# A one-core expert kernel: the pair's weighted one-hot made at its beginning, transposed inside the gate product, and the last pair's combines two k-tiles later

## The chip, the cores and the metric

The kernel runs on one core of a Trainium2 chip. The metric is the device time of one launch in microseconds (us). TensorE (PE) multiplies, VectorE (DVE), ScalarE (ACT) and GpSimd (POOL) work on tiles, SyncE (SP) issues transfers (DMA). PEld is TensorE's weight load.

## The reference

A first block of two layers and then a second block of two layers, on 256 tokens of width 1024. The change lies in the second block's expert part, which runs once in each of its two layers:

```python
def grouped_moe(h, router_w, router_bias, w_gate, w_up, w_down):
    ...
    dense_gates = jnp.einsum('nk,nke->ne', gates, jax.nn.one_hot(idx, N_EXPERTS, dtype=F32)).astype(h.dtype)
    y = jnp.zeros_like(h)
    for e in range(N_EXPERTS):
        a = jax.nn.silu(h @ w_gate[e]) * (h @ w_up[e])
        y = y + dense_gates[:, e:e + 1] * (a @ w_down[e])
    return y
```

There are 16 experts of width 512, and each token goes to two of them. All weights are float32.

## The kernel before

In `moe(l, turn)` the experts are taken in 8 pairs, and each expert of a pair has 64 slots for its tokens, so that a pair fills the 128 rows of a tile. The steps of a pair, with their lines:

- `one_hot(g, pos)` (L1546, DVE) makes a one-hot `oh` of token against slot for a group of four experts. `gather` (L1562 on PE, L1564 on ACT) multiplies it with the tokens and gives `xg`, the tokens of each slot, in 8 steps. It runs for the even pairs; an odd pair uses the same `oh` and `xg`. Some steps run ahead of the pair, the others between the k-tiles of its gate product, by the argument `more` of `proj`.
- `proj` (L1597, PE) is every product with expert weights: `pg` (gate) and `pu` (up) over `KD` = 8 k-tiles, then down over 4 k-tiles for each part of the output columns: two halves of 512, or four quarters of 256 in the last pair. Each k-tile is a matmul for each of the two experts, which work side by side in column halves of the array; the trace has two passes for each, so four matmuls.
- The activation: tanh (L1632, ACT), two products (L1633, L1634, DVE), four transposes of `a` (L1638, PE), the copy to `aT` (L1640, ACT), which the down product needs.
- `combine_T(p, oh)`: the one-hot times the token's gate (`go`, L1607, DVE, two instructions), two transposes of it (L1612, PE), and from these `got`, the 0/1 matrix of slot against token (L1615, DVE), and `gs`, the gate of each slot (L1616, DVE).
- Each part of the down product is scaled by `gs` when it is evicted: `yh` (L1671, ACT) and the rest `yl` (L1672, DVE).
- `combine` (L1655, PE) multiplies `yh` and `yl` with `got` and adds that to the state `y` (L1657, DVE). For pairs 0 to 6 it is put on the list `steps`, and `pump()` runs one part of it at each call in the next pair. In the last pair (the one with `done`, which also takes the statistics of L802) it is called by `proj` between two k-tiles, through the argument `mid`.

TensorE follows the order in which the code is written. On the other engines a scheduler sets the order, and each then works strictly in it. Weights come in slots of 1 MB from a ring of 18 or more; SP issues them (L1683) in the order of use. PSUM has four banks for products (`mm_bank`) and four for transposes and combines (`at_bank`). The loop behind the pairs (L1716) is for experts with over 64 tokens, and does not run with these inputs.

Of the kernel before, what the change touches and what calls it, by code (L numbers as in the profile page):

```python
# [23 lines left out]
KD = D // P  # L24
# [51 lines left out]
def kernel(ctx: ExitStack, tc: tile.TileContext, A, const, out):  # L76
# [15 lines left out]
    def nm(s):  # L92
        cnt[0] += 1
        return f"{s}_{cnt[0]}"

    def t512(dt=F32):
        return tmp.tile([P, 512], dt, tag="t", name=nm("t"))

    def small(w):
        return sml.tile([P, w], F32, tag=f"s{w}", name=nm("s"))  # L100

    def mm_bank():
        return pmm.tile([P, 512], F32, tag="mm", name=nm("mm"))

    def at_bank():
        return pat.tile([P, 512], F32, tag="at", name=nm("at"))
# [3 lines left out]
    def pump(n=1):  # L110

        while posts:
            posts.pop(0)()
        while n and steps:
            if next(steps[0], False) is False:
                steps.pop(0)
            else:
                n -= 1
# [389 lines left out]
    def warm(func, dep):  # L508

        S.activation(small(2)[:, 0:1], dep, func, scale=0.0, bias=epst[:, 1:2])  # L510
# [964 lines left out]
    def moe(l, turn):  # L1475
# [15 lines left out]
        done = S.activation(sc, sc, AF.Tanh, scale=0.5)  # L1491
# [17 lines left out]
        gs, key, ing, mx = [small(8).rearrange("p (a g) -> p a g", a=2) for _ in range(4)]  # L1509
# [33 lines left out]
        def one_hot(g, pos):  # L1543
            oh = sml.tile([P, 2, 4 * SLOTS], F32R, tag="oh", name=nm("oh"), bufs=2)
            for i in range(2):
                V.tensor_tensor(oh[:, i].rearrange("p (e s) -> p e s", e=4),  # L1546
                                pos[:, i, 4 * g:4 * g + 4, None].to_broadcast([P, 4, SLOTS]),
                                C("count")[:, None, :].to_broadcast([P, 4, SLOTS]), op=OP.is_equal)
            return oh

        def gather(g, oh):

            xg = unit(U_PROB[(g + 1) % 2], "xg").rearrange("p (k s) -> p k s", k=KD)
            return xg, gather_steps(xg, oh)
# [12 lines left out]
        oh = one_hot(0, pos)  # L1567
        for i in range(2):
            last = V.tensor_sub(hn[1][:, i, 512:], y[:, i, 512:], hn[0][:, i, 512:])
        xg, more = gather(0, oh)  # L1570
# [20 lines left out]

        def proj(ps, lhs, ws, nk, mid=None, more=()):
            for k in range(nk):
                if mid and k == 1:
                    mid()
                for b in range(2):
                    PE.matmul(ps[64 * b:64 * b + 64, :], lhs(k, b), ws[k][b], start=k == 0, stop=k == nk - 1)  # L1597
                if k % 2:
                    for _ in range(2):
                        next(iter(more), None)  # L1600

        def combine_T(p, oh):

            go = t512()
            o = (p % 2) * P
            for i in range(2):
                V.tensor_tensor(go[:, i * P:(i + 1) * P].rearrange("p (e s) -> p e s", e=2),  # L1607
                                oh.bitcast(F32)[:, i, o:o + P].rearrange("p (e s) -> p e s", e=2),
                                gate[:, i, 2 * p:2 * p + 2, None].to_broadcast([P, 2, SLOTS]), op=OP.mult)
            pb = at_bank()  # L1610
            for i in range(2):
                PE.transpose(pb[:, i * P:(i + 1) * P], go[:, i * P:(i + 1) * P], ident)  # L1612
            got = sml.tile([P, T], F32R, tag="got", name=nm("got"), bufs=2)
            gs = small(2)
            V.tensor_scalar(got, pb[:, :T], 0.0, None, op0=OP.is_gt)  # L1615
            V.reduce_max(gs[:, 0:1], pb[:, :T], axis=AX.X)  # L1616
            return got, gs[:, 0:1]

        def pair(p, xg, more, oh, wg, wu, wd, done=None):
            def xs(k, b):  # L1620
                o = ((2 * p + b) % 4) * SLOTS
                return xg[:, k, o:o + SLOTS]

            if done:
                got, gs = combine_T(p, oh)
            pg, pu = mm_bank(), mm_bank()
            proj(pg, xs, wg, KD, more=more)
            if done:
                pump(2)
            proj(pu, xs, wu, KD)  # L1630
            th, a = t512(), t512()
            S.activation(th, pg, AF.Tanh, scale=0.5)  # L1632
            V.scalar_tensor_tensor(th, th, 1.0, pg, op0=OP.add, op1=OP.mult)  # L1633
            V.scalar_tensor_tensor(a, th, 0.5, pu, op0=OP.mult, op1=OP.mult)  # L1634
            pump()
            pb = at_bank()
            for j in range(4):
                PE.transpose(pb[:, j * P:(j + 1) * P], a[:, j * P:(j + 1) * P], ident)  # L1638
            aT = t512()
            S.copy(aT, pb)  # L1640
            if done:
                warm(AF.Abs_reciprocal_sqrt, aT[:, 0:1])
            pump()
            if not done:
                got, gs = combine_T(p, oh)
            n = len(wd)
            w = D // n
            yos = []

            def combine():  # L1650
                for q, yo in enumerate(yos):
                    for i in range(2):
                        pc = at_bank()
                        for j, part in enumerate(yo):
                            PE.matmul(pc[:, :w], got[:, i * P:(i + 1) * P], part, start=j == 0, stop=j == 1)  # L1655
                        ys = y[:, i, w * q:w * q + w]
                        V.tensor_add(ys, ys, pc[:, :w])  # L1657
                        if done:
                            done(q, i, n=n)
                    yield  # L1660

            comb = combine()
            if not done:
                steps.append(comb)
            for q in range(n):
                pd_ = mm_bank()
                proj(pd_[:, :w], lambda k, b: aT[:, k * P + 64 * b:k * P + 64 * b + 64], wd[q], 4, lambda: done and q and next(comb))
                if w * q % 512 == 0:
                    yh, yl = t512(F32R), t512(F32R)
                sl = slice(w * q % 512, w * q % 512 + w)  # L1670
                S.activation(yh[:, sl], pd_[:, :w], AF.Copy, scale=gs)  # L1671
                V.scalar_tensor_tensor(yl[:, sl], pd_[:, :w], gs, yh[:, sl], op0=OP.mult, op1=OP.subtract)  # L1672
                yos.append((yh[:, sl], yl[:, sl]))
            if done:
                next(comb)
# [26 lines left out]
        for p in range(NPAIR):  # L1702
            if p % 2 == 0 and p > 0:
                oh = one_hot(p // 2, pos)
                xg, more = gather(p // 2, oh)
                for _ in range(4):
                    next(more)
            pair(p, xg, more, oh, *experts(p, p == NPAIR - 1), done=stats if p == NPAIR - 1 else None)
# [7 lines left out]
        with tc.For_i(1, rounds, 1):  # L1716
            V.tensor_scalar_add(pos2, pos2, -float(SLOTS))
            for p in range(NPAIR):
                if p % 2 == 0:
                    oh = one_hot(p // 2, pos2)  # L1720
                    xg, more = gather(p // 2, oh)
                    for _ in range(2):
                        next(more)
                pair(p, xg, more, oh, *experts(p))
            finish()
            for q in range(4):
                stats(q, new=False, n=4)
# [62 lines left out]
```

## Time and profile before

| | us |
|---|---|
| median of 3 runs (1618.51 to 1620.62) | 1619.72 |
| the profiled execution, its own time | 1618.68 |
| its span, first to last instruction | 1616.4 |
| PE busy | 1510.0 |
| PEld busy | 1092.7 |
| DVE busy | 976.5 |
| ACT busy | 736.3 |
| POOL busy | 251.8 |

Busy times are sums over the span, in which stages with different limits follow one another. The second block begins near 840 us (its first L1207 on ACT is at 843.7); the expert stages of the two layers lie at about 990 to 1220 us and 1372 to 1601 us, and the rest is the second block's attention part and the ends. In the expert stages the page shows DMA at 9 of 10 and over 400 GB/s; elsewhere it is lower. Matmuls are pipelined, so PE's busy time overstates what it does.

### The profile page before, as it was taken

How to read it: one execution, taken by the hardware profiler on the slowest of the kernel's cores; microseconds unless marked ns; L12 is line 12 of the kernel's file. 1: busy time of each engine (PE TensorE's matmuls, PEld its weight loads, DVE VectorE, ACT ScalarE, POOL GpSimd, SP SyncE). 2: the span in 40 equal slices, each digit the busy share in tenths (PEclk: the TensorE clock that was granted, in tenths of full speed). 3: DMA queues.
4: the chain of work that ended last, by engine and by line, in shares of the span. 5: the costliest groups of instructions: out<-in, count | busy, mean ns of one | idle time of the engine just before them, and what ended most of it. 6: DMA issues, size and time to landing. Idle time of an engine off the chain costs nothing. (4 is left out here: it accounts for less than half of the span.)

```text
span 1616.4 us, 24413 instructions
## 1 busy us (share of the span) xinstructions
PE 1510.0 (93%) x9211; PEld 1092.7 (68%) x9211; DVE 976.5 (60%) x1894; ACT 736.3 (46%) x1403; POOL 251.8 (16%) x279
## 2 busy tenths in 40 slices
PE   6999999999999999999989998999988998999996
PEld 5877888888887888888878775334437776344332
DVE  4869777777786767777557774322137767222224
ACT  3466645655456664556446664112115565111112
POOL 0334640001242363000003100000001210000000
PEclk9999999999999999999999998999998999999998
DMA  9766769557854675965526368999985558899992
GB/s 346 245 215 236 261 219 353 181 179 235 313 186 136 218 271 185 318 207 174 164 73 209 128 222 300 403 407 407 407 314 168 179 180 315 314 407 406 407 405 92
DMA packets 278476, 419.71 MB, mean 260 GB/s; under 512 B 12722, under 2 KB 147748, under 8 KB 278348
## 3 DMA queue, kind: packets, MB, share of 16 engines
q1 hardware_dynamic: 273052, 398.63, 69.5%
q0 software_dynamic: 5152, 19.14, 3.4%
q8 instruction: 77, 1.26, 0.3%
q14 instruction: 51, 0.42, 0.1%
q10 hardware_dynamic: 144, 0.26, 0.0%
HBM read 416.94 MB, written 1.05 MB: 259 GB/s over the span
## 5 line engine op out<-in xcount | busy, mean ns | idle before, releaser
L279 DVE TENSOR_TENSOR split<-raw,split 128x1024 fp32r<-128x1024 f32 (+4 forms) x330 | 411.7, 1251 | 114.3 <-ACT split L278 111.2
L289 PE MATMUL mm<-hl,split 128*128 128x512 f32 x1168 | 412.6, 397 | 0.0
L278 ACT CAST split<-raw 128x1024 fp32r<-128x1024 f32 (+4 forms) x330 | 328.7, 1000 | 131.6 <-PE mm L323 69.5
L290 PE MATMUL mm<-hl,split 128*128 128x256 f32 x1168 | 326.3, 279 | 1.0 <-DVE split L279 1.0
L289 PEld LDWEIGHTS mm<-hl,split 128*128 128x128 f32 x1168 | 219.0, 187 | 50.4 <-issue 0.7
L1597 PE MATMUL mm<-raw,xg 128*64 128x512 f32 x1024 | 230.9, 602 | 1.1 <-ACT xg L1564 1.1
L290 PEld LDWEIGHTS mm<-hl,split 128*128 128x128 f32 x1168 | 220.3, 189 | 1.5 <-DVE split L279 1.3
L1597 PEld LDWEIGHTS mm<-raw,xg 128*64 128x64 f32 x1024 | 71.5, 138 | 136.5 <-issue 118.7
L289 PE MATMUL mm<-ahl,split 128*128 128x512 f32 x352 | 123.4, 395 | 0.0
L306 ACT COPY t<-mm 128x256 f32<-128x256 f32 x152 | 56.4, 371 | 142.7 <-PE mm L290 133.7
L1597 PE MATMUL mm<-raw,t 128*64 128x512 f32 (+1 forms) x576 | 114.8, 549 | 1.4 <-ACT t L1640 1.4
L321 PE MATMUL mm<-split,hl 128*128 128x512 f32 (+4 forms) x272 | 102.3, 376 | 4.2 <-ACT split L278 3.2
L290 PE MATMUL mm<-ahl,split 128*128 128x256 f32 x352 | 98.3, 279 | 0.3 <-DVE split L279 0.3
L322 PE MATMUL mm<-split,hl 128*128 128x512 f32 (+4 forms) x272 | 96.4, 355 | 1.0 <-DVE split L279 1.0
L323 PE MATMUL mm<-split,hl 128*128 128x512 f32 (+4 forms) x272 | 96.4, 355 | 0.3 <-POOL hl L1210 0.2
L306 DVE TENSOR_TENSOR t<-mm,t 128x256 f32<-128x256 f32 x140 | 59.1, 422 | 47.9 <-ACT t L306 47.7
L1633 DVE SCALAR_TENSOR_TENSOR t<-t,mm 128x512 f32<-128x512 f32 x16 | 11.0, 686 | 123.3 <-ACT t L1632 123.3
L1597 PEld LDWEIGHTS mm<-raw,t 128*64 128x64 f32 x576 | 39.4, 137 | 63.8 <-issue 53.4
L1672 DVE SCALAR_TENSOR_TENSOR t<-mm,s,t 128x512 fp32r<-128x512 f32 (+1 forms) x36 | 24.9, 692 | 94.9 <-ACT t L1671 94.9
L1671 ACT ACTIVATE t<-mm,s 128x512 fp32r<-128x512 f32 (+1 forms) x36 | 23.0, 640 | 129.9 <-PE mm L1597 129.9
L289 PEld LDWEIGHTS mm<-ahl,split 128*128 128x128 f32 x352 | 66.0, 187 | 15.5 <-ACT t L1095 0.2
L1640 ACT COPY t<-at 128x512 f32<-128x512 f32 x16 | 9.4, 586 | 129.7 <-PE at L1638 129.7
(426 smaller groups left out, 2563.3 us busy)
## 6 DMA issues: line engine op xcount, KB each, us to landing
raw<-in_exp_w_gate_dram SPq DMA_DIRECT2D x128, 512.0 KB
raw<-in_exp_w_up_dram SPq DMA_DIRECT2D x128, 512.0 KB
raw<-in_exp_w_down_dram SPq DMA_DIRECT2D x128, 512.0 KB
raw<-in_w_in_dram SPq DMA_DIRECT2D x54, 1024.0 KB
raw<-in_w_ada_dram SPq DMA_DIRECT2D x30, 1024.0 KB
raw<-in_w_gate_dram SPq DMA_DIRECT2D x22, 1024.0 KB
raw<-in_w_up_dram SPq DMA_DIRECT2D x22, 1024.0 KB
ada<-in_w_ada_dram POOLq DMA_DIRECT2D x18, 1024.0 KB, 5.8
```

The costliest lines, as they stand in the source:

```text
L278: S.copy(h, src)
L279: V.tensor_sub(lo, src, h)
L289: PE.matmul(ps, h[:, k], x[k0 + k], start=first and k == 0, stop=False)
L290: PE.matmul(ps[:, :T], lo[:, k], x[k0 + k][:, :T], start=False, stop=last and k == K - 1)
L306: return S.copy(b[:, :T], ps[:, T:]), V.tensor_add(dst, ps[:, :T], b[:, :T])
L321: PE.matmul(ps[i][:, :n], xh, h[:, j], start=f, stop=False)
L322: PE.matmul(ps[i][:, :n], xh, lo[:, j], start=False, stop=False)
L323: PE.matmul(ps[i][:, :n], xl, h[:, j], start=False, stop=z)
L1597: PE.matmul(ps[64 * b:64 * b + 64, :], lhs(k, b), ws[k][b], start=k == 0, stop=k == nk - 1)
L1633: V.scalar_tensor_tensor(th, th, 1.0, pg, op0=OP.add, op1=OP.mult)
L1671: S.activation(yh[:, sl], pd_[:, :w], AF.Copy, scale=gs)
L1672: V.scalar_tensor_tensor(yl[:, sl], pd_[:, :w], gs, yh[:, sl], op0=OP.mult, op1=OP.subtract)
```

## The change

`combine_T` becomes a generator in two parts. The first part, `go`, is called at the beginning of every pair. The second part, the transposes with `got` and `gs`, is called by the gate product's `proj` through `mid`. And `mid` is now called ahead of the k-tile with k = 3, where it was k = 1; for the last pair's combines, which use the same argument, that is two k-tiles later. Line numbers behind L1607 grow by one to three.

```diff
@@ -1591,7 +1591,7 @@
         def proj(ps, lhs, ws, nk, mid=None, more=()):
             for k in range(nk):
-                if mid and k == 1:
+                if mid and k == 3:
                     mid()
@@ -1607,6 +1607,7 @@
                                 gate[:, i, 2 * p:2 * p + 2, None].to_broadcast([P, 2, SLOTS]), op=OP.mult)
+            yield
             pb = at_bank()
...
             V.reduce_max(gs[:, 0:1], pb[:, :T], axis=AX.X)
-            return got, gs[:, 0:1]
+            yield got, gs[:, 0:1]
...
-            if done:
-                got, gs = combine_T(p, oh)
+            turned = combine_T(p, oh)
+            next(turned)
+            box = []
             pg, pu = mm_bank(), mm_bank()
-            proj(pg, xs, wg, KD, more=more)
+            proj(pg, xs, wg, KD, lambda: box.extend(next(turned)), more)
+            got, gs = box
...
-            if not done:
-                got, gs = combine_T(p, oh)
```

TensorE in pair 1 of the first layer, before: the end of the up product (`mm_10422`), the combine of pair 0 (`at_10460` to `at_10479`) around the transposes of `a` (`at_10468`), then the transposes of the one-hot, and the first two k-tiles of the down product (`mm_10493`). Here a row x4 is two k-tiles.

```order
L1597 MATMUL mm_10422<-raw_10406,xg_10191 64x512 x4
L1655 MATMUL at_10460<-t_10368,got_10355 128x512
L1655 MATMUL at_10460<-t_10369,got_10355 128x512
L1655 MATMUL at_10464<-t_10368,got_10355 128x512
L1655 MATMUL at_10464<-t_10369,got_10355 128x512
L1638 MATMUL at_10468<-con,t_10456 128x128 x4
L1655 MATMUL at_10475<-t_10381,got_10355 128x512
L1655 MATMUL at_10475<-t_10382,got_10355 128x512
L1655 MATMUL at_10479<-t_10381,got_10355 128x512
L1655 MATMUL at_10479<-t_10382,got_10355 128x512
L1612 MATMUL at_10486<-con,t_10483 128x128 x2
L1597 MATMUL mm_10493<-raw_10409,t_10473 64x512 x4
```

The same pair of the change: first the beginning of its gate product (`mm_10424`), then the end of the same stretch as above.

```order
L1597 MATMUL mm_10424<-raw_10385,xg_10191 64x512 x4
L1597 MATMUL mm_10424<-raw_10388,xg_10191 64x512 x2
L1613 MATMUL at_10432<-con,t_10421 128x128 x2
L1597 MATMUL mm_10424<-raw_10388,xg_10191 64x512 x2
L1597 MATMUL mm_10424<-raw_10391,xg_10191 64x512 x4
```

```order
L1641 MATMUL at_10478<-con,t_10466 128x128 x4
L1656 MATMUL at_10485<-t_10381,got_10281 128x512
L1656 MATMUL at_10485<-t_10382,got_10281 128x512
L1656 MATMUL at_10489<-t_10381,got_10281 128x512
L1656 MATMUL at_10489<-t_10382,got_10281 128x512
L1597 MATMUL mm_10493<-raw_10409,t_10483 64x512 x4
```

The two transposes (L1612, now L1613) have moved from ahead of the down product to behind the third k-tile of the gate product.

VectorE from the evictions of pair 0 (`t_10369`, `t_10382`) on, before:

```order
L1672 SCALAR_TENSOR_TENSOR t_10369<-mm_10359,s_10356,t_10368 128x512
L1672 SCALAR_TENSOR_TENSOR t_10382<-mm_10372,s_10356,t_10381 128x512
L1633 SCALAR_TENSOR_TENSOR t_10455<-t_10455,mm_10421 128x512
L1634 SCALAR_TENSOR_TENSOR t_10456<-t_10455,mm_10422 128x512
L1657 TENSOR_TENSOR state_8374<-state_8374,at_10460 128x512
L1657 TENSOR_TENSOR state_8374<-state_8374,at_10464 128x512
L1657 TENSOR_TENSOR state_8374<-state_8374,at_10475 128x512
L1657 TENSOR_TENSOR state_8374<-state_8374,at_10479 128x512
L1607 TENSOR_TENSOR t_10483<-oh_10186,gate_10204 128x128 x2
L1546 TENSOR_TENSOR oh_10839<-pos_10184,con 128x256
L1615 TENSOR_SCALAR got_10489<-at_10486 128x256
L1616 TENSOR_REDUCE s_10490<-at_10486 128x1
```

And in the change:

```order
L1673 SCALAR_TENSOR_TENSOR t_10369<-mm_10359,s_10282,t_10368 128x512
L1673 SCALAR_TENSOR_TENSOR t_10382<-mm_10372,s_10282,t_10381 128x512
L1607 TENSOR_TENSOR t_10421<-oh_10186,gate_10204 128x128 x2
L1546 TENSOR_TENSOR oh_10839<-pos_10184,con 128x256 x2
L1616 TENSOR_SCALAR got_10435<-at_10432 128x256
L1617 TENSOR_REDUCE s_10436<-at_10432 128x1
L1636 SCALAR_TENSOR_TENSOR t_10465<-t_10465,mm_10424 128x512
L1637 SCALAR_TENSOR_TENSOR t_10466<-t_10465,mm_10425 128x512
L1658 TENSOR_TENSOR state_8374<-state_8374,at_10470 128x512
```

The weighted one-hot (L1607) has moved from behind the four state additions to right behind the previous pair's last eviction, and `got` and `gs` from behind the additions to ahead of the products with tanh.

TensorE in the last pair of the first layer, the first two quarters of its down product (`mm_11455`, `mm_11468`) and the first combine, before and then in the change; here a row x2 is one k-tile.

```order
L1597 MATMUL mm_11455<-raw_11369,t_11451 64x256 x8
L1597 MATMUL mm_11468<-raw_11372,t_11451 64x256 x2
L1655 MATMUL at_11471<-t_11464,got_11387 128x256
L1655 MATMUL at_11471<-t_11465,got_11387 128x256
L1655 MATMUL at_11477<-t_11464,got_11387 128x256
L1655 MATMUL at_11477<-t_11465,got_11387 128x256
L1597 MATMUL mm_11468<-raw_11372,t_11451 64x256 x6
```

```order
L1597 MATMUL mm_11455<-raw_11369,t_11451 64x256 x8
L1597 MATMUL mm_11468<-raw_11372,t_11451 64x256 x6
L1656 MATMUL at_11475<-t_11464,got_11395 128x256
L1656 MATMUL at_11475<-t_11465,got_11395 128x256
L1656 MATMUL at_11481<-t_11464,got_11395 128x256
L1656 MATMUL at_11481<-t_11465,got_11395 128x256
L1597 MATMUL mm_11468<-raw_11372,t_11451 64x256 x2
```

The combine of a quarter has moved from behind the first k-tile of the next quarter to behind its third. The last quarter's combine has no product behind it and stays where it was. ACT, POOL and SP have the same instructions in the same order.

## Rows read from the trace of the kernel before

**Rows 1.** Busy time by stretch: start:end us, length, PE, PEld, DVE, ACT, POOL, PEclk, DMA share, GB/s.

```profile
1020.00:1180.00 160.00, 152.79 (x740) 63.37 (x738) 40.09 (x75) 26.81 (x47) 0.00 (x0) 1.00 1.05 407
1221.00:1231.00 10.00, 5.83 (x23) 5.24 (x24) 5.98 (x16) 7.58 (x13) 0.78 (x3) 0.51 0.82 285
```

**Rows 2.** Groups of TensorE's matmuls from 900 us on: busy us, mean ns | idle before, releaser.

```profile
L1597 PE MATMUL mm<-raw,xg 128*64 128x512 f32 x1024 | 230.9, 602 | 1.1 <-ACT xg L1564 1.1
...
L1612 PE MATMUL at<-con,t 128*128 128x128 f32 x32 | 7.2, 305 | 18.0 <-DVE t L1607 18.0
```

**Rows 3.** TensorE's timeline in pair 2, first layer: start us, us, what.

```profile
1048.39 1.94 PE L1597 MATMUL mm<-raw,xg 128*64 128x512 f32 x8
1050.26 1.21 PE L1562 MATMUL at<-oh,hn 128*128 128x256 f32 x8
...
1054.42 10.52 PE L1597 MATMUL mm<-raw,xg 128*64 128x512 f32 x48
1064.87 1.20 PE L1655 MATMUL at<-t,got 128*128 128x512 f32 x4
1065.91 0.60 PE L1638 MATMUL at<-con,t 128*128 128x128 f32 x4
1066.27 1.17 PE L1655 MATMUL at<-t,got 128*128 128x512 f32 x4
1068.64 0.44 PE L1612 MATMUL at<-con,t 128*128 128x128 f32 x2 [1.20 <-DVE t L1607]
1069.01 7.09 PE L1597 MATMUL mm<-raw,t 128*64 128x512 f32 x32
1075.93 13.90 PE L1597 MATMUL mm<-raw,xg 128*64 128x512 f32 x64
```

**Rows 4.** The timeline of VectorE and ScalarE in the same pair.

```profile
1065.64 2.65 DVE L1657 TENSOR_TENSOR state<-state,at 128x512 f32<-128x512 f32 x4
...
1066.60 0.59 ACT L1640 COPY t<-at 128x512 f32<-128x512 f32 x1 [7.88 <-PE at L1638]
1068.21 0.48 DVE L1607 TENSOR_TENSOR t<-oh,gate 128x128 f32<-128x128 f32 x2
...
1076.87 0.75 DVE L1672 SCALAR_TENSOR_TENSOR t<-mm,s,t 128x512 fp32r<-128x512 f32 x1 [2.68 <-ACT t L1671]
```

**Rows 5.** TensorE's timeline where the last pair of the first layer begins.

```profile
1178.29 7.09 PE L1597 MATMUL mm<-raw,t 128*64 128x512 f32 x32
...
1187.61 7.09 PE L1597 MATMUL mm<-raw,xg 128*64 128x512 f32 x32
```

**Rows 6.** The timeline of the last pair's down quarters and combines, first layer.

```profile
1205.90 2.38 PE L1597 MATMUL mm<-raw,t 128*64 128x256 f32 x20 [0.68 <-ACT t L1640]
...
1208.42 1.14 PE L1655 MATMUL at<-t,got 128*128 128x256 f32 x4
1208.94 0.42 PEld L1655 LDWEIGHTS at<-t,got 128*128 128x128 f32 x3 [0.33 <-DVE t L1672]
1209.37 0.75 DVE L1657 TENSOR_TENSOR state<-state,at 128x256 f32<-128x256 f32 x2 [0.48 <-PE at L1655]
...
1209.49 1.95 PE L1597 MATMUL mm<-raw,t 128*64 128x256 f32 x16
1210.03 0.74 DVE L802 BATCH_NORM_STATS2 s<-state 128x6 f32<-128x256 f32 x2
...
1215.80 1.52 PE L1597 MATMUL mm<-raw,t 128*64 128x256 f32 x12
...
1217.89 1.14 PE L1655 MATMUL at<-t,got 128*128 128x256 f32 x4 [0.57 <-ACT t L1671]
```

**Rows 7.** TensorE's timeline in pair 0, ahead of its down product.

```profile
1014.01 0.44 PE L1612 MATMUL at<-con,t 128*128 128x128 f32 x2
1014.37 7.09 PE L1597 MATMUL mm<-raw,t 128*64 128x512 f32 x32
```

**Rows 8.** DMA busy tenths from 1180 to 1210 us, 40 slices of 0.75 us.

```profile
DMA  9999999999999999999999999999997420000000
```

## The prediction

> **What bounds the kernel now.** I read the stretches of one expert stage first, then TensorE's order of time inside it, then what the pauses there wait for. In the expert stage the DMA share is full (1.05) and TensorE is busy for 152.8 of 160 us [rows 1]. Both cannot set the pace, so the next thing to see is which waits. The gate and up products, 1024 matmuls in both layers, have 1.1 us of idle time before them, and none of it is put down to DMA; the pair's two transposes (L1612), 32 in both layers, have 18.0 us, all put down to L1607, the weighted one-hot on VectorE [rows 2]. TensorE's work therefore sets the stage, with the weights close ahead of it, and the time lost in it is of two kinds.
>
> The first is in the middle of a pair [rows 3, 4]. The up product ends, the older pair's first combine half runs at 1064.87, four transposes of `a` at 1065.91, the second combine half at 1066.27. The down product then needs only `aT`, whose copy ends at 1066.60 + 0.59 = 1067.19. But L1612 stands ahead of it and waits for L1607, which stands on VectorE behind the four state additions (2.65 us from 1065.64). So L1612 starts at 1068.64 and the down product at 1069.01.
>
> The second kind is in the last pair [rows 5, 6]. Its gate product starts at 1187.61 behind the same wait, and its combines follow the eviction of their own quarter so closely that each stalls twice: the first matmul at 1208.42 waits for ACT's high part, the second waits until 1208.94 for VectorE's low part.
>
> **Unit prices.** A chain of 48 product matmuls takes 1064.87 - 1054.42 = 10.45 us to the next kind of matmul, a chain of 8 takes 1050.26 - 1048.39 = 1.87 [rows 3]. The difference, 8.58 us for 40, is 0.2145 us each (a k-tile is four, 0.86), and the chain of 8 has 1.87 - 1.72 = 0.15 us that belongs to no matmul: the price of entering and leaving a chain. Two transposes take 1069.01 - 1068.64 = 0.37 to the next product. Splitting the gate product for them therefore costs 0.37 + 0.15 = 0.52 us. The bounds are 0.37 (no price for the split) and 0.67 (two such prices). I take 0.52, since the 0.15 was read on the same pair of shapes.
>
> The Trainium skill has a rule that speaks against this place: in TensorEngine Tiling (Array Packing), section Key Properties, a change of the tiling mode drains TensorE, and the product runs in 128x64 tiles while the transposes use the whole array. The trace agrees that there is a price, and puts it at 0.15 us a chain; the page gives none. A large drain is the slower rival below.
>
> **Pairs 1 to 6 (each layer).** Without L1612 the down product follows the second combine half. Four such matmuls take 1065.91 - 1064.87 = 1.04 us, so it starts at 1066.27 + 1.04 = 1067.31, and `aT` is there before. That is 1.70 us earlier. Minus 0.52 in the gate product: 1.18 us net, 7.08 for six.
>
> Is the wait only moved? L1607 now stands on VectorE right behind the previous pair's last eviction. That eviction is 1076.87 + 0.75 = 1077.62 in the trace, so L1607 would end at 1077.62 + 0.48 = 1078.10 [rows 4]. The gate product began at 1075.93, and three k-tiles later is 1078.50. The cover is thus the first three k-tiles of the gate product, with 0.4 us to spare in the odd pairs and in the last; the even pairs gather first and have more. If that cover went, everything behind the transposes on TensorE (the other five k-tiles, and through them tanh on ACT) would wait. `got` on VectorE now waits for transposes in mid-product; behind it stands only the product with tanh, which cannot run before the gate product is done. The next one-hots (L1546) run ahead of `got`, and nobody waits for them there. No DMA is moved: SP, GpSimd and ACT keep their order.
>
> **Pair 0.** It had no wait: L1612 takes 0.36 us (1014.01 to 1014.37) ahead of the down product [rows 7]. It loses 0.52 and gets back between 0 and 0.36, as the down product may wait for `aT`; I take 0.3. Net -0.2.
>
> **Last pair, gate product.** Its predecessor's down product starts at 1178.29 [rows 5] and such a chain of 32 takes 1075.93 - 1069.01 = 6.92, so the gate product could start at 1185.21 in place of 1187.61. That is 2.40, minus 0.52: 1.88.
>
> **Last pair, combines.** Here k-tiles are half as wide: 16 matmuls are busy 1.95, 12 are busy 1.52 [rows 6], so four cost 0.43. The three combine matmuls that no longer wait take 1209.49 - 1208.94 = 0.55; with the first, 0.67. Now the first combine starts after 28 matmuls in place of 20: 1205.90 + 28 x 0.1075 + 0.15 = 1209.06. High and low parts are there by 1208.94, so it runs through. The next comes after 0.67 + 16 x 0.1075 + 0.15 = 2.54, the third at 1214.14. Then 0.67, and the last k-tile, from whose start the old tail counts: today 1215.80 to 1217.89 holds 12 matmuls, so 4 need 2.09 - 0.86 = 1.23. The final combine is at 1216.04, not 1217.89: 1.85. What is late next is VectorE: additions start 0.43 after a combine's second matmul, and statistics (0.74) start 0.66 after the additions, so those of the third combine end near 1216.1 and hold the last low part by some 0.1. I take 1.8 (1.4 if this delay hits each quarter).
>
> **Sum.** 7.08 - 0.2 + 1.88 + 1.8 = 10.56 us a layer, 21.1 for two. The profiled execution took 1618.68 us (its span of 1616.4 and 2.3 around it); that gives 1597.6. The median of the runs is 1.04 higher, so I predict 1598.6.
>
> By the bounds: with 0.37 a split, 0.36 back in pair 0 and 1.9 for the combines, 8.0 + 0 + 2.0 + 1.9 = 11.9 a layer, 1595.9. With 0.67, another 0.15 before the down product, nothing back in pair 0 and 1.4, 5.3 - 0.7 + 1.7 + 1.4 = 7.7, 1604.3. After each stage the clock is at its lower level, 1.2 GHz, for some ten us (0.51 granted from 1221 to 1231, after TensorE had paused [rows 1]). TensorE is busy 5.8 us of that; where the shifted stage meets this is not in the trace, and can be worth 2 us either way.
>
> **Rivals.**
> *The weights become the bound.* DMA stays full until about 1202.5 [rows 8], whatever TensorE does. The last quarter's first k-tile would be wanted at 1214.14 - 0.1 - 1.29 = 1212.75, less the 8.76 gained by then: 1204.0. So 1.5 us is left, more for earlier pieces, and part of what is in that row is the next stage's weights. For it: the margin shrinks from some 10 us to 1.5. Against: it stays positive. If transfers ended 5 us later, 3.5 us a layer would be lost: 1605.6.
>
> *The wait moves along.* If the transposes waited 1.20 us in the gate product, as they do now, pairs 1 to 6 would give 6 x (1.70 - 0.52 - 1.20) = -0.1 and the last 0.7: with the combines some 2.2 a layer, 1615.3. Against it is the 0.4 us cover; for it, that the cover is small.
>
> *Slower: leaving the tiled product in its middle is dear.* Without any price for the 16 splits the sum is 0.3 + 10.2 + 2.4 + 1.8 = 14.7 a layer, 29.4. It turns at 1.84 us a split. At 2.5 us, from weight loads that can no longer run ahead, it is 16 x 2.5 - 29.4 = 10.6 slower: 1630.3. For it: the trace has no product that is left and entered again with nothing else to do in between than two transposes. Against: the chains of 8 are left and entered just so for the gathers, and lose 0.15 [rows 3].
>
> **How the numbers follow.** My forecast has 0.80, the weights 0.08, the moved wait 0.06, the dear split 0.03, and 0.03 is left for a gain that the next stage swallows. The forecast's own bounds and the clock give 1594 to 1606, which takes in the weights' 1605.6 and leaves the moved wait and the slower case out. A measurement of this kernel can tell about 0.2% (3.2 us) from no change. Forecast, weights and most of the moved wait are faster by more: 0.93. No change 0.03, slower 0.04.
>
> **What would show it.** The transposes' group should have almost no idle time; the down product should start about 1.04 us after the second combine half; the last pair's gate product should start within 0.2 us of the end of the down product before it; its combines should be 2.5 us apart (3.16 now); from first gather to last combine the stage should be 10.5 us shorter. I am wrong if the wait for L1607 stands again before the transposes in the gate product, if a weight load of the last pair waits for DMA, or if the eight product matmuls around the transposes lose over 1 us.

## The result and the profile after

| | before | after |
|---|---|---|
| median of 4 runs, us | 1619.12 (1615.14 to 1620.62) | 1598.85 (1597.79 to 1600.17) |
| ratio, 95% interval | | 0.9879 (0.9859 to 0.9898) |
| profiled execution, us | 1618.68 | 1598.5 |
| its span, us | 1616.4 | 1596.3 |
| stage of the first layer, us | 228.44 | 217.87 |
| stage of the second layer, us | 228.38 | 217.80 |

The forecast was 1598.6 us. A stage is counted from the first gather of its first pair to the beginning of the last combine; in the first layer TensorE's timeline has the two starts at 989.45 and 1217.89 before, at 990.61 and 1208.48 after. Both stages are 10.57 and 10.58 us shorter, where the sum said 10.56. Both together are 21.15 us; the span fell by 20.1, because the first stage began 1.16 us later, and what runs ahead of it is not touched by the change.

First the two views with which the reading of before began. The transposes' group in the grouped view of after (busy time, mean ns of one | idle time before them):

```profile
L1613 PE MATMUL at<-con,t 128*128 128x128 f32 x32 | 7.0, 301 | 0.0
```

Before, the same 32 transposes had 18.0 us of idle time in front of them [rows 2]; now they have none. The windows of after, with the columns of [rows 1]:

```profile
1020.00:1180.00 160.00, 159.94 (x772) 64.51 (x770) 41.39 (x77) 27.79 (x49) 0.00 (x0) 1.00 1.05 407
1210.00:1221.00 11.00, 5.25 (x21) 4.66 (x21) 6.23 (x18) 7.21 (x12) 0.89 (x3) 0.53 0.76 260
```

TensorE was busy 152.79 of these 160 us [rows 1]; now it is busy throughout, at the same DMA share. That answers what set the pace: TensorE's order did, and the transfers kept up.

TensorE's timeline of after, from the gate product of pair 2 to the first combine half of pair 3 (start, us, engine, line, operation, count, idle before):

```profile
1054.75 10.52 PE L1597 MATMUL mm<-raw,xg 128*64 128x512 f32 x48
1065.20 1.20 PE L1656 MATMUL at<-t,got 128*128 128x512 f32 x4
1066.23 0.60 PE L1641 MATMUL at<-con,t 128*128 128x128 f32 x4
1066.59 1.18 PE L1656 MATMUL at<-t,got 128*128 128x512 f32 x4
1067.70 7.09 PE L1597 MATMUL mm<-raw,t 128*64 128x512 f32 x32
1074.61 2.75 PE L1597 MATMUL mm<-raw,xg 128*64 128x512 f32 x12
1077.29 0.44 PE L1613 MATMUL at<-con,t 128*128 128x128 f32 x2
1077.66 11.38 PE L1597 MATMUL mm<-raw,xg 128*64 128x512 f32 x52
1088.97 1.19 PE L1656 MATMUL at<-t,got 128*128 128x512 f32 x4
```

From the first combine half to the down product it is 2.50 us (1065.20 to 1067.70), and was 4.14 [rows 3]. The gate and up chain with the transposes in it takes 14.36 us (1074.61 to 1088.97). And from the beginning of the last pair:

```profile
1172.60 7.09 PE L1597 MATMUL mm<-raw,t 128*64 128x512 f32 x32
1179.52 2.74 PE L1597 MATMUL mm<-raw,xg 128*64 128x512 f32 x12
1182.19 0.44 PE L1613 MATMUL at<-con,t 128*128 128x128 f32 x2
...
1198.33 3.24 PE L1597 MATMUL mm<-raw,t 128*64 128x256 f32 x28 [0.72 <-ACT t L1643]
1201.50 0.74 PE L1656 MATMUL at<-t,got 128*128 128x256 f32 x4
1202.17 1.95 PE L1597 MATMUL mm<-raw,t 128*64 128x256 f32 x16
1204.05 0.73 PE L1656 MATMUL at<-t,got 128*128 128x256 f32 x4
...
1208.48 1.14 PE L1656 MATMUL at<-t,got 128*128 128x256 f32 x4 [0.57 <-ACT t L1672]
```

The gate product follows the down product at once (6.92 us behind its start), with no wait for the one-hot [rows 5]. The combines run through in 0.67 us, 2.55 us apart; they took 1.07 us before, with stalls of their inputs [rows 6]. The last one still waits 0.57 us for its eviction, as before.

### The profile page after: what moved, and what is told of

It reads as the page before. It is cut to its first block, busy times and chain, and to the rows that moved or that the text cites. A ratio compares the mean times of both kernels' runs of the same rounds, so it can differ in the third digit from the quotient of the medians.

```text
span 1596.3 us, 24445 instructions
## 1 busy us (share of the span) xinstructions
PE 1508.8 (95%) x9211; PEld 1091.9 (68%) x9211; DVE 977.2 (61%) x1894; ACT 736.9 (46%) x1403; POOL 251.3 (16%) x279
## 3 DMA queue, kind: packets, MB, share of 16 engines
HBM read 416.94 MB, written 1.05 MB: 262 GB/s over the span
## 5 line engine op out<-in xcount | busy, mean ns | idle before, releaser
L289 PEld LDWEIGHTS mm<-ahl,split 128*128 128x128 f32 x352 | 65.9, 187 | 15.0 <-ACT t L1095 0.2
L290 PEld LDWEIGHTS mm<-ahl,split 128*128 128x128 f32 x352 | 66.5, 189 | 0.6 <-DVE split L279 0.6
```

Source lines behind the costliest of these rows:

```text
L289: PE.matmul(ps, h[:, k], x[k0 + k], start=first and k == 0, stop=False)
L290: PE.matmul(ps[:, :T], lo[:, k], x[k0 + k][:, :T], start=False, stop=last and k == K - 1)
```

## The experiments

All were timed beside the kernel before, 1620.94 us in the first four, 1618.71 in the last three. The table puts the stages of both layers (counted as above) beside the times.

| kernel | median, us | ratio to before (95%) | stages, us |
|---|---|---|---|
| transposes moved, combines as before | 1606.51 | 0.9902 (0.9884 to 0.9920) | 220.11, 219.69 |
| combines moved, transposes as before | 1617.22 | 0.9977 (0.9966 to 0.9988) | 226.13, 226.25 |
| transposes two k-tiles earlier | 1611.67 | 0.9942 (0.9925 to 0.9959) | 224.27, 224.24 |
| transposes behind the up product | 1599.55 | 0.9860 (0.9839 to 0.9882) | 218.01, 218.01 |
| gathers halved | 1592.67 | 0.9836 (0.9817 to 0.9855) | 215.06, 216.04 |
| transposes in two places, none in a product | 1594.20 | 0.9859 (0.9838 to 0.9880) | 215.03, 214.91 |
| the changed kernel again | 1600.46 | 0.9890 (0.9871 to 0.9908) | 218.20, 217.98 |

**Each half of the change alone.** The first kernel is the changed one with the last combines ahead of k = 1 again; the second is the kernel before with one line changed.

```diff
-        def proj(ps, lhs, ws, nk, mid=None, more=()):
+        def proj(ps, lhs, ws, nk, mid=None, more=(), at=3):
-                if mid and k == 3:
+                if mid and k == at:
...
-                proj(pd_[:, :w], ..., lambda: done and q and next(comb))
+                proj(pd_[:, :w], ..., lambda: done and q and next(comb), at=1)
```

```diff
-                if mid and k == 1:
+                if mid and k == 3:
```

> The moved transposes alone; the last pair's combines stay behind the first k-tile of the next quarter. My sum: pairs 1 to 6 give 7.1 us a layer, pair 0 takes 0.2, the last pair's gate product gives 1.9, so 17.5 us of the 21.1: about 1601.6 against 1619.1 before. If the gain came mostly from the last pair's combines, this run would be within a few us of the kernel before. In its profile the combines of the last pair are 3.16 us apart and wait twice each, as in the kernel before, and the transposes of the one-hot have no idle time before them.

> The kernel before with the last pair's combines two k-tiles later and nothing else. My sum: 1.8 us a layer, 3.6 in all, about 1615.5 against 1619.1 before; combines 2.54 us apart in place of 3.16. If VectorE were the bound of these quarters (it evicts, adds and takes statistics in order), the distance would stay near 3 us and the time within 1 us of the kernel before.

The first stage is 8.33 us shorter with the transposes alone and 2.31 with the combines alone, 10.64 together; the change has 10.57. In the second layer it is 8.69 and 2.13, 10.82 together, and 10.58. So the two halves hardly help or hinder each other, and the product of the two ratios (0.9902 x 0.9977 = 0.9879) is that of the change. The combines alone took 3.7 us off the median, where 3.6 had been expected. In TensorE's timeline of the combines alone, the last down product and the last combine:

```profile
1210.57 3.24 PE L1597 MATMUL mm<-raw,t 128*64 128x256 f32 x28 [0.68 <-ACT t L1640]
...
1220.72 1.14 PE L1655 MATMUL at<-t,got 128*128 128x256 f32 x4 [0.57 <-ACT t L1671]
```

That is 10.15 us, the same as in the changed kernel (1198.33 to 1208.48), and was 11.99 [rows 6]: 1.84 us for this term; the other 0.48 of the 2.31 lie in pair 0, which this kernel does not change. The transposes alone did not reach their forecast in total time, though they did in the stages. The windows show where much of the rest is: first of the transposes alone, then of the changed kernel run again.

```profile
900.00:923.00 23.00, 22.38 (x149) 18.18 (x147) 14.29 (x37) 11.56 (x35) 0.54 (x1) 1.00 0.38 137
923.00:931.00 8.00, 8.00 (x44) 5.75 (x43) 4.92 (x16) 5.53 (x16) 2.47 (x4) 0.57 0.32 91
1298.00:1306.00 8.00, 8.00 (x39) 5.47 (x37) 4.86 (x16) 4.68 (x16) 3.01 (x4) 0.57 0.14 29
```

```profile
923.00:931.00 8.00, 7.40 (x54) 5.05 (x54) 6.49 (x19) 6.73 (x22) 3.01 (x4) 1.00 0.25 61
```

In the attention part of both layers, far from the change, TensorE was granted 0.57 of its clock for 8 us (that is, most of the time the lower level, 1.2 GHz), and 1.00 in the other kernel. In the 23 us ahead of the first of them it had been busy for 22.38. The first stage of that execution began at 992.87, 3.4 us later than before, and the second one 155.9 us after the last combine of the first, in place of 154.0. Those 5.3 us are about what is missing: the profiled execution took 1606.85 us, 11.8 less than before, where its two stages gave 17.0. Some 1.8 of them came with the first fall and 1.9 with the second; 1.6 had come ahead of both, since the last L1207 on ACT starts at 854.10 there and at 852.53 before. Why the clock fell stays open. It is not a matter of this kernel alone: in the first layer the traces of three other kernels below (transposes two k-tiles earlier, gathers halved, transposes in two places) have 0.57 to 0.59 from 921 to 929 us. The other five runs of this kernel have no trace, so the clock is shown as the cause for the profiled execution and only likely for the median.

**The cover taken away.** The changed kernel, with the transposes ahead of k = 1 of the gate product (`at` as in the first kernel):

```diff
-            proj(pg, xs, wg, KD, lambda: box.extend(next(turned)), more)
+            proj(pg, xs, wg, KD, lambda: box.extend(next(turned)), more, at=1)
```

> The change with the one-hot's transposes behind the first k-tile of the gate product, not the third; the combines of the last pair as in the change. It asks whether the three k-tiles are what covers the one-hot. My reading: in the odd pairs and the last pair the one-hot is ready about 2.1 us after the gate product's start, the transposes are due after 1.0, so TensorE waits about 1.1 us in four pairs a layer and some 0.7 in pair 0; even pairs gather first and don't wait. That is 5.1 us a layer, about 1609 against 1598.9 of the change. If the one-hot had no such cover and the place inside the product did not matter, the time would be that of the change within 1 us.

Its transposes in the grouped view, and TensorE's timeline at the beginning of pair 1:

```profile
L1613 PE MATMUL at<-con,t 128*128 128x128 f32 x32 | 7.7, 321 | 9.7 <-DVE t L1607 7.9 <-DVE nri L1587 1.8
```

```profile
1024.31 1.03 PE L1597 MATMUL mm<-raw,xg 128*64 128x512 f32 x4
1026.25 0.53 PE L1613 MATMUL at<-con,t 128*128 128x128 f32 x2 [0.92 <-DVE t L1607]
```

The wait for L1607 is back, 7.9 us of it in both layers, and a stage is 6.4 us longer than in the changed kernel, where 5.1 had been expected. In an odd pair the transposes are due 1.0 us after the gate product began and start at 1.94 (pair 1) to 2.03; behind three k-tiles they start at 2.68 and do not wait. From one down product to the next an odd pair then takes 24.84 us: of the 1.12 that the change gives it (24.89 before, 23.77 after) 0.05 is left. The even pairs gather first, do not wait, and keep all of theirs (28.61). The four odd pairs, the last one among them, make 4.3 us; the other 2.1 are pair 0's, where 0.7 had been expected. Its transposes wait 0.90 us, by the view for the end of the routing (`nri`, L1587), and the lower clock lasts longer there. The same stretch of this kernel, then of the changed one:

```profile
990.60:1000.00 9.40, 8.40 (x28) 4.41 (x29) 6.42 (x23) 1.80 (x4) 0.00 (x0) 0.53 0.23 78
```

```profile
990.60:1000.00 9.40, 9.21 (x36) 4.49 (x37) 6.47 (x23) 2.17 (x4) 0.00 (x0) 0.74 0.45 159
```

The second layer has the same, 0.50 granted in place of 0.73 in the 9.40 us from its first gather. The longer wait and the longer lower clock come together in both layers; that the one makes the other is not shown by a run of its own.

The three k-tiles are the cover, as the prediction had it, with 0.6 us to spare rather than 0.4. VectorE's row in pair 3 of the changed kernel, whose gate product begins at 1074.61 and whose transposes start at 1077.29, has the one-hot done at 1076.70:

```profile
1076.22 0.48 DVE L1607 TENSOR_TENSOR t<-oh,gate 128x128 f32<-128x128 f32 x2
```

Of pair 0 the prediction had not said that they cover anything.

**No split at all: behind the up product.** The changed kernel, with the transposes ahead of the combine instead of in the gate product:

```diff
-            proj(pg, xs, wg, KD, lambda: box.extend(next(turned)), more)
-            got, gs = box
+            proj(pg, xs, wg, KD, more=more)
...
             V.scalar_tensor_tensor(a, th, 0.5, pu, op0=OP.mult, op1=OP.mult)
+            got, gs = next(turned)
             pump()
```

> The change with the one-hot's transposes taken out of the gate product and put behind the up product, next to the combine of the older pair, where TensorE leaves the tiled product anyway. It asks what the split of the gate product costs. My price for a split is 0.52 us, of which 0.37 are the two transposes with the way back and 0.15 the second entering and leaving of a product. Beside other whole-array matmuls they should cost about 0.25. In pairs 1 to 6 that gives 0.27 each, less up to 0.15 because got and gs now stand on VectorE ahead of the state additions and the fourth combine matmul pair waits for the first addition's bank; in pair 0 and the last pair, where TensorE waits 0.8 us for the product with tanh at that place, the whole 0.52. Sum 1.7 to 2.6 us a layer: 1593.6 to 1595.5 against 1598.9 of the change. If a split is free, the time is that of the change, or slower by what VectorE adds.

The stages did not change, so this forecast failed. TensorE and VectorE at pair 2:

```profile
1066.11 0.44 PE L1613 MATMUL at<-con,t 128*128 128x128 f32 x2
1066.30 1.17 PE L1655 MATMUL at<-t,got 128*128 128x512 f32 x4
1067.32 0.60 PE L1640 MATMUL at<-con,t 128*128 128x128 f32 x4
1067.72 0.70 PE L1655 MATMUL at<-t,got 128*128 128x512 f32 x2
1068.63 0.74 PE L1655 MATMUL at<-t,got 128*128 128x512 f32 x2 [0.20 <-ACT t L1642]
1069.30 7.09 PE L1597 MATMUL mm<-raw,t 128*64 128x512 f32 x32
```

```profile
1066.83 0.42 DVE L1616 TENSOR_SCALAR got<-at 128x256 fp32r<-128x256 f32 x1
1067.16 0.41 DVE L1617 TENSOR_REDUCE s<-at 128x1 f32<-128x256 f32 x1
1067.50 2.60 DVE L1657 TENSOR_TENSOR state<-state,at 128x512 f32<-128x512 f32 x4
```

The transposes are cheap here, 0.19 us. But `got` and `gs` now stand on VectorE ahead of the state additions, which begin at 1067.50, 1.20 us after the combine's first matmul (0.77 in the changed kernel: 1065.97 and 1065.20). The second combine half then falls into two pieces: its last two matmuls start at 1068.63, and the down product 1.58 us after the half's beginning in place of 1.11. Their weight load, and ACT's row there:

```profile
1068.63 0.30 PEld L1655 LDWEIGHTS at<-t,got 128*128 128x128 f32 x2 [0.64 <-ACT t L1642]
```

```profile
1067.99 0.59 ACT L1642 COPY t<-at 128x512 f32<-128x512 f32 x1 [8.04 <-PE at L1640]
```

The load starts 0.05 us after ACT's copy to `aT` ends (1067.99 + 0.59 = 1068.58), and over 0.4 after the first state addition was done (about 1068.2). So it is the copy that ends this wait, and not the addition that the forecast had named. The combine takes no data from that copy. What fits is the PSUM bank that the copy reads, one of four, now that the one-hot's transposes take one of them in the middle of the pair; no run tests that. From one down product to the next the odd pairs take 23.9 us and the even ones 28.8, some 0.2 more than in the changed kernel: the 0.53 that the split cost is lost again, and a little more. Pair 0 and the last pair, where TensorE waits for tanh anyway, did gain (the last 0.58), so the stage as a whole stays.

**No split: two places.** From that follows a kernel that takes the good place of each pair: behind the product with tanh for pair 0 and the last, and behind the second combine half for the others, where `got` stands behind the state additions.

```diff
-            proj(pg, xs, wg, KD, lambda: box.extend(next(turned)), more)
-            got, gs = box
+            proj(pg, xs, wg, KD, more=more)
...
             V.scalar_tensor_tensor(a, th, 0.5, pu, op0=OP.mult, op1=OP.mult)
+            if p == 0 or done:
+                got, gs = next(turned)
             pump()
...
                 warm(AF.Abs_reciprocal_sqrt, aT[:, 0:1])
             pump()
+            if p and not done:
+                got, gs = next(turned)
```

> The changed kernel with its weighted one-hot still made at the pair's beginning, but the two transposes in no product: in pair 0 and the last pair right behind the product with tanh is asked for (in the pause in which TensorE waits for it), in pairs 1 to 6 behind the second combine half, where the kernel before had them. Theory 1 (an early one-hot is all that the old place lacked, and the split in the gate product costs 0.15 us beyond the transposes' own 0.37): 0.15 us less in each of six pairs, about 0.5 less in pair 0 and in the last, 1.9 a layer, 3.8 in all: near 1595, with the transposes starting right behind the combine and no wait on L1607. Theory 2 (a split costs nothing, or the old place waits for a PSUM bank of the state additions): pairs 1 to 6 gain nothing or lose, 0 to 1 us a layer in all, 1597 to 1600. Should the weights of layer 1 (2.0 us ahead) become the bound, up to 1 us of the gain is lost there.

> The changed kernel unchanged, as the base for the two beside it on the same chip: 1597 to 1601, stages of about 218.7 us from first gather to last combine, and a ratio to the kernel before near 0.988.

The stages are 3.17 and 3.07 us shorter than those of the changed kernel beside it, the median is 6.3 us lower (one of its five runs took 1600.51), and the first theory had 1.9 a layer. In the first layer pairs 1 to 6 give 1.90 (0.9 in the theory), pair 0 0.72 and the last pair 0.55 (0.5 each). TensorE at pair 2:

```profile
1064.84 1.20 PE L1658 MATMUL at<-t,got 128*128 128x512 f32 x4
...
1066.23 1.18 PE L1658 MATMUL at<-t,got 128*128 128x512 f32 x4
1067.25 0.38 PE L1613 MATMUL at<-con,t 128*128 128x128 f32 x2
1067.56 7.09 PE L1597 MATMUL mm<-raw,t 128*64 128x512 f32 x32
1074.48 13.90 PE L1597 MATMUL mm<-raw,xg 128*64 128x512 f32 x64
1088.31 1.20 PE L1658 MATMUL at<-t,got 128*128 128x512 f32 x4
```

The gate and up chain is back to 13.83 us (1074.48 to 1088.31), 0.53 less. The transposes put the down product only 0.22 us later (2.72 behind the first combine half, 2.50 in the changed kernel), and not 0.37. They follow the combine without a pause (1067.25, 1.02 behind the second half's beginning), and the product follows them after 0.31. In the changed kernel the product itself starts 1.11 behind that beginning (1066.59 to 1067.70), so 0.09 goes by between the combine and the product there too. The 0.37 thus held a step from whole-array matmuls into the product that the old place pays anyway; 0.31 - 0.09 = 0.22 is what the transposes add. So a pair gains 0.53 - 0.22 = 0.31, not 0.15.

The loads' view puts the wait of the changed kernel's product down to ACT's copy to `aT`. The load in pair 2, then the copy there and in the last pair:

```profile
1067.69 0.20 PEld L1597 LDWEIGHTS mm<-raw,t 128*64 128x64 f32 x4 [0.37 <-ACT t L1643]
```

```profile
1066.91 0.59 ACT L1643 COPY t<-at 128x512 f32<-128x512 f32 x1 [7.87 <-PE at L1641]
1197.69 0.59 ACT L1643 COPY t<-at 128x512 f32<-128x512 f32 x1 [9.97 <-PE at L1641]
```

In the last pair TensorE has nothing else to do, and the product (1198.33) follows the copy's end (1198.28) by 0.05 us. In pair 2 the copy ended at 1067.50, 0.20 us ahead of the product, so there it is not what the product waited for, and the transposes do not lie in a wait for it.

**What stands next behind TensorE.** The changed kernel with the low part of the gathers left out, so its result is less exact:

```diff
-                for q in range(2):
+                for q in range(1):
...
-                        PE.matmul(..., start=n == 0, stop=n == 3)
+                        PE.matmul(..., start=n == 0, stop=n == 1)
```

> The changed kernel with the low part of the expert gathers left out (one of the two products for each gathered tile), so its output is not the reference's: it asks what stands next behind TensorE. A gather matmul of the low part is 0.115 us or so and there are 64 of them a layer: TensorE's own work falls by about 7.4 us a layer, 14.8 us in all. Theory 1 (TensorE still sets the stage after the change, with the weights of the last pair 2 to 3 us ahead): the gain is cut off where the last quarter of the last pair's down weights lands; with 2.9 us of margin in layer 0 and 2.0 in layer 1 that is about 5 us in all, near 1594, and the last pair's matmuls wait for DMA on their weight loads. Theory 2 (the weights already hold the changed kernel): no gain, 1598 to 1600, waits for DMA in the last pair of the changed kernel already. Theory 3 (weights far behind the need): the whole 14.8 us, near 1584, no wait for DMA.

TensorE's timeline at the last pair of the first layer, and the waits of its weight loads there (us in total, times, longest):

```profile
1166.34 7.09 PE L1597 MATMUL mm<-raw,t 128*64 128x512 f32 x32
1173.26 3.49 PE L1597 MATMUL mm<-raw,xg 128*64 128x512 f32 x12
1176.67 0.44 PE L1613 MATMUL at<-con,t 128*128 128x128 f32 x2
1177.04 5.70 PE L1597 MATMUL mm<-raw,xg 128*64 128x512 f32 x20
...
1205.35 1.13 PE L1656 MATMUL at<-t,got 128*128 128x256 f32 x4 [0.57 <-ACT t L1672]
```

```profile
PEld mm L1597 <- DMA raw<-in_exp_w_gate_dram: 2.4, 6, 1.0
...
PEld mm L1597 <- DMA raw<-in_exp_w_up_dram: 1.5, 3, 1.0
```

From the first gather (990.29) to pair 6's down product the stage takes 176.05 us, and 181.99 in the changed kernel: 5.94 gained, where 7.4 had been expected of the gathers. From there to the last combine it takes 39.01 in place of 35.88 and gives 3.13 back, because the last pair's gate and up pieces arrive no sooner. So the weights do stand next: in the changed kernel they were ahead of TensorE's need by 2.8 us in the first layer and, by what its stage gained, by 1.8 in the second. The two stages together hold 4.6 to 5.1 us of the median's 7.8; 1.9 more is that the first one began earlier than in the kernel beside it (992.15). Theory 1 holds, but for the piece: gate and up of the last pair bind, not the down quarter from which its margins and the forecast's rival were worked out.

## Why the prediction was right

- **The pace.** TensorE's work set the stage, and the DMA share of 1.05 did not: TensorE went to 159.94 of 160 us at the same share.
- **Pairs 1 to 6:** 1.18 each was forecast. From one down product to the next, the odd pairs take 23.77 us (1067.70 to 1091.47 in the trace; 24.89 before) and the even ones 28.62 (29.74): 1.12 each. The split costs 14.36 - 13.83 = 0.53 (forecast 0.52). The shortfall is the down product, 1.11 behind the second combine half's beginning in place of 1.04. `aT` is there before, as the text had said (1067.50, and 1066.59 + 1.04 = 1067.63). The 1.04 was read from the combine to other whole-array matmuls, and the step into the product comes on top. In pair 6 of the first layer the product starts 1.24 behind; there the copy to `aT` ends at 1172.55, 0.05 ahead of it, and is what it waits for. The six give 6.63 where 7.08 was forecast.
- **Pair 0:** -0.2 forecast, +0.22 measured (24.92 us from first gather to down product before, 24.70 after). In the second layer it is 0.05 (24.83 and 24.78). The stage begins in a stretch at the lower clock (0.50 to 0.51 granted from 989.45 to 995.45 in both kernels), and the later it begins in it, the less of it is spent there. In the second trace of the same kernel this part took 25.05. The term is below what the clock moves here, so the 0.42 over the forecast cannot be put down to the change.
- **Last pair:** 1.88 forecast for the gate product; from pair 6's down product to the last one it is 25.73 us in place of 27.61, 1.88. The combines: 1.8 forecast, 1.84 measured.
- **The sum.** 10.57 against 10.56 is closer than its terms are. Pairs 1 to 6 fell 0.45 short and pair 0 gave 0.42 more than forecast; that the two cancel is luck. The total is lucky as well: the median fell by 20.3 us and not by 21.1, from a median of before that lay 0.6 below the one that the forecast started from.
- **The clock behind the stage:** granted 0.53 from 1210 to 1221, and 0.51 from 1221 to 1231 before [rows 1]. The stretch came along with the stage: from the last combine of the first stage to the first gather of the second it is 154.03 us in both kernels.
- **The rivals.** That the wait moves along is what two k-tiles less make true, in the odd pairs. A dear split is ruled out by 0.53 us. Of these, 0.31 is what leaving the product and entering it again costs, since the same two transposes add 0.22 where no product is split. The Trainium skill says in TensorEngine Tiling (Array Packing), section Key Properties, that a change of tiling mode drains TensorE; the trace agrees in that there is a price, and 0.31 us is small. The weights did not bind, with 2.8 us to spare, where 1.5 had been estimated for another piece. One sign of being wrong did appear by its letter: in the changed kernel the loads' view puts two waits for gate weights in the last pair down to DMA. They are 0.3 us each, no longer than the gaps of loads that wait for nothing, and the matmuls around them lost nothing (2.74 and 4.51 us for 12 and 20).

## What to carry to other kernels

A producer that stands late on an in-order engine is best made early, but its consumer must be put behind enough work to cover it: here one k-tile in front kept 0.05 of an odd pair's 1.12 us, and three kept all. Before an independent instruction is put into a long chain, look for a wait in which it costs nothing, since the split price (0.53 us) was avoided by two other places, one of them such a wait, and 6.3 us more came of it. And ask of each place what the instructions behind it then wait for: behind the up product the transposes cost 0.19 us, but half of the second combine then waited for ACT's copy, and all that the cheaper place had saved was given back.

## What was not expected of the hardware

The granted clock can spoil a comparison of totals: one execution ran 8 us at 0.57 in each layer's attention part while TensorE was busy 8.00 of 8 us, and another kernel with the same code there had 1.00; some 1.9 us went with each such stretch. Stages between two named instructions agreed within 0.4 us in the two traces of the changed kernel, where the totals of one kernel's runs differed by 2.4 to 7.6 us. A wait that a view puts down to an engine is worth a look at that engine's row: TensorE's product followed ACT's copy by 0.05 us where it did wait for it, and by 0.20 where the copy was merely the last thing that the view knew of. A weight load that waits is not always shown as idle time of the matmul behind it: with the gathers halved, 32 matmuls took 9.19 us (3.49 and 5.70) in place of 7.25 and only the loads' view names DMA.
